# One layer of a hybrid gated-DeltaNet / GLA trunk on one core: weight block sums made by accumulating transfers, and a decay gate in one pass

## The chip, the cores and the metric

The kernel runs on one core of a Trainium2 chip. The metric is the device time of one execution in microseconds (us), the median of several runs. The engines are named as the profile names them: PE is TensorE (PEld its weight loads), DVE is VectorE, ACT is ScalarE, POOL is GpSimd, SP is SyncE, whose queue issues most transfers.

## The reference, cut to what matters

One layer over 1024 frames of width 1024, all in fp32. One input projection feeds two branches, and only the second one's gate is written out here:

```python
h = rmsnorm(x, norm_mix_g)                      # (1024, 1024)
# w_in: columns of every head group
gdn: q, k, v, z, decay, beta                    # gated DeltaNet, 8 heads of 128
gla: q, k (4 heads of 128), v, r (4 heads of 256), low (rank 16)
merge gates: two of width 1024
...
gk = log_sigmoid(low @ gla_w_gate2 + bias) / 16 # the decay gate, (1024, 512)
o_gla = gla_chunked(q, k, v, gk)                # a scan over chunks of the state
x += merge(gdn, gla) @ w_out
x += cross_attention(x, mem)                    # 4 heads, 256 memory tokens
x += relu(rmsnorm(x) @ w1) ** 2 @ w2
```

Most of the arithmetic is in plain matrix products: the input projection, the output projections, and the two of the MLP.

## The kernel before, in words

An fp32 product is made of three single-pass matmuls (`mm3`, L582, L584, L586): each operand is split into a high part, which ACT rounds off (L622), and a low part, the difference, which DVE or POOL makes (L623); the passes are high by high, high by low and low by high. Where a matmul takes fp32 operands as they are, TensorE makes several passes of it by itself (L1067 in the decay gate, L1138 to L1142 in the scan).

Large dense products are also cut into 2 x 2 blocks and made with seven block products in place of eight (`wino`, `gla_dense`). The activations' block sums are made once (`bs`). The weights' block sums are made again for every weight unit, that is for every 256 columns of a weight: two `raw` tiles hold its blocks A11, A12, A21, A22, each of 128 x 512 elements, and `wino_w` adds and subtracts blocks in place (L1751, L1752, L1754, L1756), on POOL in the code. A planner may give such an instruction to DVE, and mostly does. Each of the seven operands is split into a tile of the ring `wop`, which has four tiles (RING). Twelve matmuls make one block product on 512 columns: four tiles of the contraction by three passes.

The stage that the change is about is `phase_gla`, the gated heads' stage, from about 100 to 650 us. For each of four heads it projects q, k, v and r, and makes the decay gate (`gla_gate`: one product of rank 16, as two matmuls of 512 columns, and then a log-sigmoid and a running sum), the scores (`gla_scores`), the scan over eight chunks (`gla_scan`), the norm and the output. Between these the code takes steps from a queue of dense products (`push`, `fill`, `until`; FA to FJ say how many), which hold the head's own projections and also the DeltaNet heads' q, k, v and z, by the table EXTRA. The DeltaNet stage follows, from about 650 to 1105 us, with dense products between its steps too (FILL, TFILL, SFILL).

The order on each engine is not the code's: the planner orders all instructions by a cost table, and the DMA queues' too. Every engine then works through its own list and waits where an operand or a buffer is not ready. The scan's squares (L1152) write to the tile `th`, of which there is one buffer, and keep only the sum. `pd` and `ps` are four banks each of the matmul accumulator; `ex` and `dx` are rows of 128 x 1024.

Of the kernel before, what the change touches and what calls it, by code (L numbers as in the profile page):

```python
# [11 lines left out]
F32 = mybir.dt.float32  # L12
# [6 lines left out]
P = 128  # L19
D = 1024  # L20
T = 1024
# [45 lines left out]
EXTRA = (('v', 'k', 't', 'q'), ('v', 't', 'k', 'q'), ('v', 't', 'k', 'q'), ('v', 't', 'k', 'q'))  # L67
QB, FOLDB = 2, 1
SFILL, PFILL, TFILL = 5, (2, 12), (4, 14, 0, 8, 10, 10)
FILL = ((7,), ('z0', 6, 10, 'z6', 'Q2'), (9, 'O1', 'z5', 'z3', 'Q3', 'z1'), ('z2', 'z4', 14, 'O0', 11, 'O3', 'z7', 8, 'Q1'), ('O2', 13, 'Q0', 12))  # L70
LASTG = (15, 5)
LAYP = (('PF', 8192, 1), ('k1', 4096, 2), ('NT1', 4096, 2), ('NT0', 4096, 2), ('Pm', 4096, 1), ('dm', 4096, 2), ('k0', 4096, 2), ('kdt0', 4096, 2), ('kdt1', 4096, 2), ('pr', 1024, 1), ('q', 4096, 2))
LAYQ = (('AT', 4096, 2), ('v0', 4096, 2), ('acc', 2048, 2), ('sz', 2048, 2), ('v1', 4096, 2), ('X', 4096, 2))
# [15 lines left out]
class Op:  # L89
# [7 lines left out]
    def __init__(self, ins, flex):  # L97
# [33 lines left out]
        if ins.opcode == "DMACopy":  # L131
            self.dma, self.cost, self.own, self.lat = True, ISSUE, LAND, LAND
            self.bytes = n * 4 * outs[0].ap[0][1]
            if ins_[0].bass_ap.tensor.name in HEADIN:
# [366 lines left out]
class Layer:  # L501
# [428 lines left out]
    def joined(self, dest, done=None, scale=1.0):  # L930

        nc = self.nc

        def put(b, pt):
            nc.scalar.activation(dest(*b), pt, AF.Copy, scale=scale)  # L935

        def add(b, pt):
            o = dest(*b)
            if scale == 1.0:
                nc.vector.tensor_tensor(o, pt, o, ADD)  # L940
            else:
                nc.vector.scalar_tensor_tensor(o, pt, scale, o, MUL, ADD)
# [12 lines left out]
        return evict  # L955

    def gla_dense(self, evicts, after=None):

        n, ws = self.wino_w(range(7), GLOV)
        yield  # L960
        bank = self.banks(2)
        for p in range(7):
            if p == 3:
                self.fetch_w()
# [18 lines left out]
    def gla_qk(self, sp):  # L983
        qk = [self.til(sp, [P, T], "qk", bufs=2) for _ in range(2)]
        return qk, self.joined(lambda i, half: qk[i][:, half * HALF:(half + 1) * HALF], None, float(P) ** -0.25)

    def push_gla_v(self, sp, h):

        v = [self.til(sp, [P, NB, 256], "v", bufs=2) for _ in range(2)]

        def dest(e):
            return lambda i, half: v[i][:, 4 * half + 2 * e:4 * half + 2 * e + 2].rearrange("p a b -> p (a b)")

        self.push(f"v{h}", self.gla_dense([[self.joined(dest(e)) for e in range(2)]]))
        return v

    def push_gla_r(self, sp, h, after=None):

        nc = self.nc
        sr = [self.dxt(sp) for _ in range(2)]  # L1000

        def done(j, half, o, x):
            nc.scalar.activation(o, x, AF.Silu)

        self.push(f"r{h}", self.gla_dense([self.joined(lambda j, half: sr[j][:, half * HALF:(half + 1) * HALF], done)],
                                          after))
        return sr

    def push_pair(self, sp, x, after=None):
# [8 lines left out]
        def done(i, half, o, x_):  # L1018
            nc.scalar.activation(o, x_, AF.Silu)
            nc.sync.dma_start(self.gd["z", u][i][:, half * HALF:(half + 1) * HALF], o)  # L1020

        self.push(x, self.gla_dense([self.joined(dest, done)], after))

    def push_qv(self, sp, which, u, after=None):
# [9 lines left out]
        def done(i, half, o, src):  # L1034
            if o is not src:
                nc.scalar.activation(o, src, AF.Copy)
# [19 lines left out]
        self.push(f"g{which}{u}", self.gla_dense([self.joined(dest, done)], after))  # L1056
        return turn()

    def gla_gate(self, sp, h):
        nc = self.nc  # L1060
        w2 = self.til(sp, [96, P], "w2g", bufs=1)
        nc.sync.dma_start(w2, self.a["w2g"][:, h * P:(h + 1) * P])
        zb = self.ext(sp)
        for half in range(2):
            s = slice(half * HALF, (half + 1) * HALF)
            pt = self.pss()
            nc.tensor.matmul(pt, w2, self.sm[:96, s], start=True, stop=True)  # L1067
# [121 lines left out]
    def queue_gla(self):  # L1189
# [5 lines left out]
        for h in range(LH):  # L1195
# [3 lines left out]
            q += [[a[f"w_g{x}"][h] if len(x) == 1 else a["w_gz"][int(x[1])]]  # L1199
# [3 lines left out]
    def phase_gla(self):  # L1203
        nc, a = self.nc, self.a
        with ExitStack() as ctx:
            sp = self.pool(ctx, "pgla", "right", bufs=2)
            self.bs[3] = self.late_h(self.t1d, lambda: self.ext(sp))
            sm = self.sm = self.til(sp, [P, T], "sm", bufs=1)
            g4 = self.dxt(sp)

            def done(i, half, o, x):
                if i == 1:
                    nc.scalar.activation(o, x, AF.Tanh, scale=0.5)
# [4 lines left out]
                                                        done), ev]))  # L1218
            self.until("u0")
            v = self.push_gla_v(sp, 0)  # L1220
# [506 lines left out]
    def fetch_w(self):  # L1727
# [3 lines left out]
        n, srcs = self.wq.popleft()  # L1731
        rs = []
        for src in srcs:
            rs.append([self.til(self.wp, [P, n, 256], "raw", bufs=RAWS) for _ in src])
            for t, x in zip(rs[-1], src):
                self.load(t, x)
        self.wr.append((n, rs))

    def wino_w(self, order, lov):
# [4 lines left out]
        n, rs = self.wr.popleft()  # L1744
# [627 lines left out]

def _rows(w, n):
# [5 lines left out]
def _layout(i):  # L2379
# [8 lines left out]
    A["w_lqk"] = _pairs(w[:, np.concatenate([np.concatenate([lq[h * P:(h + 1) * P], lk[h * P:(h + 1) * P]])  # L2388
                                             for h in range(LH)])])
    A["w_lv"] = _pairs(w[:, lv])  # L2390
    A["w_lr"] = _pairs(w[:, lr])
    for x, c in (("k", gk), ("q", gq), ("z", gz), ("v", gv)):
        A[f"w_g{x}"] = _pairs(w[:, c])

    gate = np.concatenate([ta, tb])
    A["w_gate"] = _units(w, gate, 16)
    sg = np.zeros((D, 256), w.dtype)
    sg[:, 0:8], sg[:, 32:40], sg[:, 64:80], sg[:, P:] = w[:, ga], w[:, gb], w[:, lg], w[:, gate[4 * P:5 * P]]
    A["w_gzd"] = _units(w, gz, 8)
    A["w_sg"] = _pairs(sg)  # L2400
    w2g = np.zeros((96, 512), w.dtype)
    w2g[64:80] = i["gla_w_gate2"][0]
# [58 lines left out]
```

## Time and profile before

| | |
|---|---|
| time, median of three runs | 2117.42 us (2116.35 to 2118.87) |
| profiled execution | 2117.52 us, of which its span is 2115.8 us |
| granted TensorE clock | 0.999 |
| busy, share of the span | PE 99%, PEld 84%, DVE 75%, ACT 57%, POOL 7% |
| DMA queues | 329.50 MB in 158235 packets, a mean of 156 GB/s |

A row of busy times gives, for each engine, the microseconds in which it worked and the count of its instructions. A row of waits reads: the engine that waited, the tile and line that it was about to work on, the engine, tile and line that it waited for, the total in us, how many times, and the longest. A row of a group gives line, engine, operation, output tile, input tiles and shape, the count, busy us, mean ns of one, the idle time ahead of it and what ended that. A row of the timeline begins with start and duration in us. Matmuls are pipelined, so the distance between two starts, not the duration, is what one costs.

### The profile page before, as it was taken

What the parts mean: (1) busy time and instruction counts of PE and PEld (TensorE: products, weight loads), DVE (VectorE), ACT (ScalarE), POOL (GpSimd) and SP (SyncE); (2) the same over time, 40 slices, a digit from 0 to 9 for tenths busy, and PEclk for the clock granted to TensorE, in tenths of its full rate; (3) what the DMA queues carried; (4) which work ended last, traced back from release to release, by engine and by line L of the source; (5) the groups of instructions that cost most, each with busy time, mean ns of one, the idle gap of its engine ahead of it and who ended that gap; (6) DMA issues with size and microseconds to landing.
All of it is one profiled execution on the core that took longest, in us unless ns stands there. A gap on an engine that the chain in (4) does not pass through costs nothing. (4 is left out here: it accounts for less than half of the span.)

```text
span 2115.8 us, 30952 instructions
## 1 busy us (share of the span) xinstructions
PE 2095.9 (99%) x10946; PEld 1783.7 (84%) x10946; DVE 1591.4 (75%) x2824; ACT 1210.2 (57%) x2390; POOL 158.3 (7%) x175
## 2 busy tenths in 40 slices
PE   8999999999999999999999999999999999999998
PEld 8889888898888899889888888888788888888887
DVE  8858888848776978787569999479967567567755
ACT  7446666637646586665655456566755557444433
POOL 0000001000001323231000000000100000000000
PEclk9999999999999999999999999999999999999999
DMA  8322232312325344554587752226444447778752
GB/s 329 129 71 63 90 106 83 93 61 95 100 95 199 116 133 135 187 171 140 176 281 244 257 169 88 90 73 221 137 146 141 156 151 213 220 250 293 248 180 100
DMA packets 158235, 329.50 MB, mean 156 GB/s; under 512 B 17016, under 2 KB 25592, under 8 KB 158080
## 3 DMA queue, kind: packets, MB, share of 16 engines
q1 hardware_dynamic: 157936, 327.50, 46.8%
q8 instruction: 86, 1.41, 0.3%
q14 instruction: 69, 0.57, 0.1%
q10 hardware_dynamic: 144, 0.03, 0.0%
HBM read 227.29 MB, written 100.17 MB: 155 GB/s over the span
## 5 line engine op out<-in xcount | busy, mean ns | idle before, releaser
L622 ACT ACTIVATE wop<-raw 128x512 fp32r<-128x512 f32 (+1 forms) x520 | 337.9, 654 | 431.4 <-PE pd L586 191.7
L623 DVE TENSOR_TENSOR wop<-raw,wop 128x512 fp32r<-128x512 f32 (+1 forms) x496 | 348.6, 706 | 232.3 <-ACT wop L622 224.7
L582 PE MATMUL pd<-t,wop 128*128 128x512 f32 x332 | 130.3, 393 | 0.5 <-ACT t L622 0.5
L586 PE MATMUL pd<-t,wop 128*128 128x512 f32 x332 | 130.4, 393 | 0.0
L584 PE MATMUL pd<-t,wop 128*128 128x512 f32 x332 | 130.2, 392 | 0.0
L584 PE MATMUL pd<-A1b,wop 128*128 128x512 f32 x272 | 106.3, 391 | 0.0
L582 PE MATMUL pd<-A1b,wop 128*128 128x512 f32 x272 | 105.9, 390 | 0.0
L586 PE MATMUL pd<-A1b,wop 128*128 128x512 f32 x260 | 101.2, 390 | 0.0
L1269 DVE SCALAR_TENSOR_TENSOR dx<-dx,convw,dx 128x1023 f32<-128x1023 f32 (+2 forms) x72 | 90.8, 1278 | 2.8 <-ACT dx L1267 2.5
L584 PE MATMUL pd<-A1a,wop 128*128 128x512 f32 x208 | 81.7, 393 | 0.0
L582 PE MATMUL pd<-A1a,wop 128*128 128x512 f32 x208 | 81.4, 391 | 0.0
L586 PE MATMUL pd<-A1a,wop 128*128 128x512 f32 x196 | 76.8, 392 | 0.0
L582 PEld LDWEIGHTS pd<-t,wop 128*128 128x128 f32 x332 | 62.3, 188 | 14.0 <-ACT t L622 0.9
L584 PEld LDWEIGHTS pd<-t,wop 128*128 128x128 f32 x332 | 62.4, 188 | 13.1 <-DVE t L623 0.4
L586 PEld LDWEIGHTS pd<-t,wop 128*128 128x128 f32 x332 | 62.4, 188 | 12.8
L622 ACT ACTIVATE whi<-raw 128x512 fp32r<-128x512 f32 x70 | 43.0, 626 | 34.8 <-PE pd L584 12.7
L582 PEld LDWEIGHTS pd<-A1b,wop 128*128 128x128 f32 x272 | 51.1, 188 | 10.7 <-ACT wop L622 0.3
L584 PEld LDWEIGHTS pd<-A1b,wop 128*128 128x128 f32 x272 | 51.1, 188 | 10.6 <-DVE A1b L623 0.2
L586 PEld LDWEIGHTS pd<-A1b,wop 128*128 128x128 f32 x260 | 48.8, 188 | 9.9
L623 DVE TENSOR_TENSOR wlo<-raw,whi 128x512 fp32r<-128x512 f32 x66 | 45.2, 685 | 14.3 <-ACT whi L622 12.3
L582 PEld LDWEIGHTS pd<-A1a,wop 128*128 128x128 f32 x208 | 39.1, 188 | 8.3 <-ACT dx L935 0.3
L584 PEld LDWEIGHTS pd<-A1a,wop 128*128 128x128 f32 x208 | 39.1, 188 | 8.0
(646 smaller groups left out, 6502.3 us busy)
## 6 DMA issues: line engine op xcount, KB each, us to landing
raw<-in_w_dram SPq DMA_DIRECT2D x120, 256.0 KB, 3.6
raw<-in_w_dram SPq DMA_DIRECT2D x32, 512.0 KB, 3.7
e<-ad SPq DMA_DIRECT2D x63, 256.0 KB, 4.6
ad<-q SPq DMA_DIRECT2D x45, 256.0 KB, 2.7
rawa<-ad SPq DMA_DIRECT2D x42, 256.0 KB, 4.4
A0b<-tgd SPq DMA_DIRECT2D x32, 256.0 KB, 5.2
ad<-acc SPq DMA_DIRECT2D x30, 256.0 KB, 2.3
ad<-u SPq DMA_DIRECT2D x30, 256.0 KB, 2.6
```

Source lines behind the costliest of these rows:

```text
L582: nc.tensor.matmul(out, lh, rh, start=first and i == 0, stop=False, skip_group_check=True)
L584: nc.tensor.matmul(out, lh, rl, start=False, stop=False, skip_group_check=True)
L586: nc.tensor.matmul(out, ll, rh, start=False, stop=last and i == n - 1, skip_group_check=True)
L622: nc.scalar.activation(hi, raw, AF.Copy)
L623: (lo_eng or nc.gpsimd).tensor_tensor(lo, raw, hi.bitcast(F32), SUB)
L1269: self.nc.vector.scalar_tensor_tensor(y[:, d:], x[:, :T - d], cw[:, 3 - d:4 - d], y[:, d:], MUL, ADD)
```

## The change

It has two parts, and numbers that were set anew with them.

First, in `phase_gla` the weights' block sums are made by transfers. `gla_w` takes the place of `wino_w` there: a block is read from memory a second time, by a transfer that POOL's queue issues and that adds to what stands in the tile. The sums that are wanted are now sums only: A21 becomes A21 + A22, then + A11, then + A12, and A11 becomes A11 + A21, in the order of products 0, 1, 3, 2, 4, 5, 6. The signs that this needs are put into the splits of products 2, 3 and 6 (ACT with a scale of -1, DVE with a scalar_tensor_tensor), and the lower halves of the outputs come out negated, which the evictions turn round (`low`). The weights are laid out by blocks in memory (`_blocks`), so that a block is one contiguous run in each partition. The product stages outside `phase_gla` keep `wino_w`.

Second, the decay gate's product: `low` holds the low-rank rows three times, in rows 48, 64 and 96, where the projection's weight (`w_sg`) has them three times. One copy of them is made a low part (rows 32 to 64 less their rounded value), two stay rounded; the gate's weight `w2` has the rounded value in rows 48 and 64 and its low part in row 96. So one single-pass matmul over 128 rows adds up low by high, high by high and high by low. `w2` is loaded into the tile `th`, and then copied and subtracted.

Third, FD, FH, FJ, EXTRA, SFILL, TFILL, FILL, LASTG, LAYP and LAYQ (fill numbers, the order of dense products, and the layout of two pools) have new values. `push_pair` can also make the merge gates, but EXTRA does not use that.

```diff
-FA, FB, FC, FD, FE, FG, FH, FI = 23, 31, 30, 20, 47, 24, 2, 0
+FA, FB, FC, FD, FE, FG, FH, FI = 23, 31, 30, 28, 47, 24, 0, 0
-FJ = 12
+FJ = 24
-EXTRA = (('v', 'k', 't', 'q'), ('v', 't', 'k', 'q'), ('v', 't', 'k', 'q'), ('v', 't', 'k', 'q'))
+EXTRA = (('v', 'k', 't', 'q'), ('v', 't', 'k', 'q'), ('k', 'v', 't', 'q'), ('k', 'v', 't', 'q'))
...
-    def joined(self, dest, done=None, scale=1.0):
+    def joined(self, dest, done=None, scale=1.0, low=1.0):
...
-            nc.scalar.activation(dest(*b), pt, AF.Copy, scale=scale)
+            nc.scalar.activation(dest(*b), pt, AF.Copy, scale=scale * (low if b[0] else 1.0))
...
+            elif f == -1.0:
+                nc.vector.tensor_tensor(o, o, pt, SUB)
...
+    SUMS = (0, 1, 3, 2, 4, 5, 6)
+
+    def gla_w(self):
...
+        more = lambda dst, src: nc.gpsimd.dma_start(dst, src, accum_op=ADD)
+        for p in self.SUMS:
+            for o, (a, src) in zip(ops, bl):
+                A11, A12, A21, A22 = a
+                if p == 0:
+                    more(A21, src[3])
...
+                w, (hi, lo) = (A11, A12, A21, A21, A11, A21, A22)[p], o[p]
+                if p in (2, 3, 6):
+                    nc.scalar.activation(hi, w, AF.Copy, scale=-1.0)
+                    nc.vector.scalar_tensor_tensor(lo, w, -1.0, hi.bitcast(F32), MUL, SUB)
+                else:
+                    self.split(w, hi, lo, nc.vector if p in GLOV else None)
+                if p in (0, 2, 3):
+                    more(*{0: (A11, src[2]), 3: (A21, src[0]), 2: (A21, src[1])}[p])
+        return n, ops
...
-        n, ws = self.wino_w(range(7), GLOV)
+        n, ws = self.gla_w()
...
     def gla_gate(self, sp, h):
         nc = self.nc
-        w2 = self.til(sp, [96, P], "w2g", bufs=1)
-        nc.sync.dma_start(w2, self.a["w2g"][:, h * P:(h + 1) * P])
+        raw = self.til(self.tp, [P, HALF], "th", bufs=THB)[:, :P]
+        nc.sync.dma_start(raw, self.a["w2g"][:, h * P:(h + 1) * P])
+        w2 = self.til(sp, [P, P], "w2g", F32R, bufs=1)
+        nc.scalar.activation(w2, raw, AF.Copy)
+        nc.vector.tensor_tensor(w2[96:], raw[96:], w2[96:].bitcast(F32), SUB)
...
-            nc.tensor.matmul(pt, w2, self.sm[:96, s], start=True, stop=True)
+            nc.tensor.matmul(pt, w2, self.low[:, s], start=True, stop=True)
...
-            sm = self.sm = self.til(sp, [P, T], "sm", bufs=1)
+            sm = self.sm = self.dxt(sp)
+            self.low = self.til(sp, [P, T], "sm", F32R, bufs=1)
...
+            nc.scalar.activation(self.low, sm, AF.Copy)
+            nc.vector.tensor_tensor(self.low[32:64], sm[32:64], self.low[32:64].bitcast(F32), SUB)
```

What this moves is seen at three places. In these rows a line is that of its own kernel (L622 of before is L624 of after, L623 is L625, L582 is L584, L1067 is L1111), and numbers behind a tile's name only tell its instances apart. The first place is DVE in head 2, where the q and k weights are split and summed (`raw`, `wop`), with the DeltaNet heads' convolution (`dx`) between. Before:

```order
L1752 TENSOR_TENSOR raw_3643<-raw_3643 128x4x128
L623 TENSOR_TENSOR wop_3722<-raw_3644,wop_3722 128x512
L1104 COPY ge_3865<-ex_3251 128x8
L1756 TENSOR_TENSOR raw_3644<-raw_3644,raw_3643 128x4x128
L940 TENSOR_TENSOR dx_3614<-pd_3647,dx_3614 128x512
L623 TENSOR_TENSOR wop_3727<-raw_3643,wop_3727 128x512
L1269 SCALAR_TENSOR_TENSOR dx_3688<-dx_3614,convw_194,dx_3688 128x1023
L623 TENSOR_TENSOR wop_3730<-raw_3643,wop_3730 128x512
L1269 SCALAR_TENSOR_TENSOR dx_3688<-dx_3614,convw_194,dx_3688 128x1022
L1754 TENSOR_TENSOR raw_3643<-raw_3644,raw_3643 128x4x128
```

After, for the same unit, products 3, 2 and then 4 and 5:

```order
L987 SCALAR_TENSOR_TENSOR wop_3739<-raw_3657,wop_3739 128x512
L1316 SCALAR_TENSOR_TENSOR dx_3700<-dx_3626,convw_194,dx_3700 128x1023
L1316 SCALAR_TENSOR_TENSOR dx_3700<-dx_3626,convw_194,dx_3700 128x1022
L1316 SCALAR_TENSOR_TENSOR dx_3700<-dx_3626,convw_194,dx_3700 128x1021
L1316 SCALAR_TENSOR_TENSOR dx_3722<-dx_3655,convw_194,dx_3722 128x1023
L1316 SCALAR_TENSOR_TENSOR dx_3722<-dx_3655,convw_194,dx_3722 128x1022
L987 SCALAR_TENSOR_TENSOR wop_3743<-raw_3657,wop_3743 128x512
L625 TENSOR_TENSOR wop_3747<-raw_3657,wop_3747 128x512
L946 SCALAR_TENSOR_TENSOR qk_3239<-pd_3770,qk_3239 128x512
```

The sums on `raw` (L1752, L1754, L1756) are gone from DVE, and the splits that wait for transfers (L987) stand there with other work between them. The second place is POOL's list, over the same part of the stage and a little around it. Before:

```order
L1756 TENSOR_TENSOR raw_3334<-raw_3334,raw_3333 128x4x128
L1751 TENSOR_TENSOR raw_3500<-raw_3500,raw_3501 128x4x128
L623 TENSOR_TENSOR wop_3441<-raw_3333,wop_3441 128x512
L1121 MEMSET ex_3848 64x4x64 x2
L1124 AFFINE_SELECT ex_3848<-ex_3848 128x512 x2
```

After, with the transfers of two weight units interleaved:

```order
L625 TENSOR_TENSOR wop_3450<-raw_3348,wop_3450 128x512
L972 DMA raw_3347<-in_w_gk_dram 128x512 x2
L972 DMA raw_3514<-in_w_gq_dram 128x512 x2
L972 DMA raw_3657<-in_w_lqk_dram 128x512
L972 DMA raw_3514<-in_w_gq_dram 128x512
L972 DMA raw_3657<-in_w_lqk_dram 128x512 x3
L972 DMA raw_3798<-in_w_lv_dram 128x1024
```

Where POOL had one block operation now and then, its list now holds four transfers for each unit, 92 in all, each of which waits in the list for the split ahead of it. The third place is PE at the decay gate of head 1, right behind the scan of head 0. Before, from the scan's last two matmuls, with ten dense matmuls up to the gate:

```order
L1140 MATMUL ps_2246<-v_1532,ex_1692 128x256
L1142 MATMUL ps_2246<-S_2237,qk_1281 128x256
L586 MATMUL pd_2040<-t_154_1159,wop_2037 128x512
L582 MATMUL pd_2040<-t_154_1159,wop_2037 128x512
L584 MATMUL pd_2040<-t_154_1159,wop_2037 128x512
L586 MATMUL pd_2040<-t_154_1159,wop_2037 128x512
L582 MATMUL pd_2040<-t_154_1159,wop_2037 128x512
L584 MATMUL pd_2040<-t_154_1159,wop_2037 128x512
L586 MATMUL pd_2040<-t_154_1159,wop_2037 128x512
L582 MATMUL pd_2040<-t_154_1159,wop_2037 128x512
L584 MATMUL pd_2040<-t_154_1159,wop_2037 128x512
L586 MATMUL pd_2040<-t_154_1159,wop_2037 128x512
```

```order
L1067 MATMUL ps_2278<-sm_1279,w2g_2275 128x512
L1067 MATMUL ps_2281<-sm_1279,w2g_2275 128x512
L582 MATMUL pd_2329<-A0a_202,wop_2304 128x512
L584 MATMUL pd_2329<-A0a_202,wop_2304 128x512
L586 MATMUL pd_2329<-A0a_202,wop_2304 128x512
```

After, the last rows ahead of the gate, and the gate:

```order
L588 MATMUL pd_2046<-t_154_1159,wop_2043 128x512
L584 MATMUL pd_2338<-A0a_202,wop_2314 128x512
L586 MATMUL pd_2338<-A0a_202,wop_2314 128x512
L588 MATMUL pd_2338<-A0a_202,wop_2314 128x512
L584 MATMUL pd_2338<-A0a_202,wop_2314 128x512
L1111 MATMUL ps_2287<-sm_1280,w2g_2283 128x512
L1111 MATMUL ps_2290<-sm_1280,w2g_2283 128x512
L586 MATMUL pd_2338<-A0a_202,wop_2314 128x512
```

The gate stands 28 dense matmuls behind the scan now (10 before), four of which already belong to the next product (`pd_2338`), and its two rows are of the single-pass kind.

More of the change, by code (lines that the diff above doesn't have):

```diff
@@ L992, in dest @@
             return lambda i, half: v[i][:, 4 * half + 2 * e:4 * half + 2 * e + 2].rearrange("p a b -> p (a b)")
-        self.push(f"v{h}", self.gla_dense([[self.joined(dest(e)) for e in range(2)]]))
+        self.push(f"v{h}", self.gla_dense([[self.joined(dest(e), None, 1.0, -1.0) for e in range(2)]]))
         return v
@@ L1002, in done @@
         def done(j, half, o, x):
-            nc.scalar.activation(o, x, AF.Silu)
-        self.push(f"r{h}", self.gla_dense([self.joined(lambda j, half: sr[j][:, half * HALF:(half + 1) * HALF], done)],
-                                          after))
+            nc.scalar.activation(o, x, AF.Silu, scale=1.0 if x is o else -1.0)
+        self.push(f"r{h}", self.gla_dense([self.joined(lambda j, half: sr[j][:, half * HALF:(half + 1) * HALF], done,
+                                                       1.0, -1.0)], after))
         return sr
@@ L1018, in done @@
         def done(i, half, o, x_):
-            nc.scalar.activation(o, x_, AF.Silu)
-            nc.sync.dma_start(self.gd["z", u][i][:, half * HALF:(half + 1) * HALF], o)
-        self.push(x, self.gla_dense([self.joined(dest, done)], after))
+            f = 1.0 if x_ is o else -1.0
+            if x[0] == "z":
+                nc.scalar.activation(o, x_, AF.Silu, scale=f)
+            else:
+                nc.scalar.activation(o, x_, AF.Tanh, scale=0.5 * f)
+            nc.sync.dma_start((self.gd["z", u][i] if x[0] == "z" else self.tgd[2 * u + i])[:, half * HALF:(half + 1) * HALF], o)
+        self.push(x, self.gla_dense([self.joined(dest, done, 1.0, -1.0)], after))
     def push_qv(self, sp, which, u, after=None):
@@ L1054, in turn @@
                     yield
-        self.push(f"g{which}{u}", self.gla_dense([self.joined(dest, done)], after))
+        self.push(f"g{which}{u}", self.gla_dense([self.joined(dest, done, 1.0, -1.0)], after))
         return turn()
@@ L1731, in fetch_w @@
         n, srcs = self.wq.popleft()
+        srcs = [[x for x in src] for src in srcs]
         rs = []
         for src in srcs:
-            rs.append([self.til(self.wp, [P, n, 256], "raw", bufs=RAWS) for _ in src])
+            rs.append([self.til(self.wp, list(x.shape), "raw", bufs=RAWS) for x in src])
             for t, x in zip(rs[-1], src):
                 self.load(t, x)
-        self.wr.append((n, rs))
+        self.wr.append((n, rs, srcs))
     def wino_w(self, order, lov):
```

66 lines of the change are left out of this document (43 added, 23 removed).

## The prediction

> **What bounds the kernel now.** I read the page first, then PE's list of waits, then the stretches by window.
>
> ```profile
> span 2115.8 us, 30952 instructions
> PE 2095.9 (99%) x10946; PEld 1783.7 (84%) x10946; DVE 1591.4 (75%) x2824; ACT 1210.2 (57%) x2390; POOL 158.3 (7%) x175
> ```
>
> PE is busy 2095.9 of 2115.8 us; every other engine has room. The profiled execution took 2117.52 us, so 1.7 us lie outside its span; it stands 0.1 us from the median of the three runs (2117.42), so what I subtract from the one can be subtracted from the other. The list of PE's waits says where the 20 us without a matmul are:
>
> ```profile
> PE pd L582 <- ACT mT L736: 5.6, 1, 5.6
> PE ps L1443 <- DVE NT L1366: 1.5, 1, 1.5
> PE pd L582 <- ACT q L935: 1.4, 1, 1.4
> PE ps L1443 <- ACT PF L1431: 1.3, 1, 1.3
> ```
>
> The largest is the start of the program. None lies in the stage that is changed: by the windows (PE's busy time is the first pair behind the length, then PEld, DVE, ACT, POOL, the granted clock, the DMA share and GB/s), PE is busy in all of 100 to 650 us, the gated heads' stage, and misses 4.87 us in 650 to 1105, the DeltaNet stage. The third row is a stretch of plain dense products.
>
> ```profile
> 100.00:650.00 550.00, 550.00 (x2973) 469.51 (x2972) 420.77 (x608) 325.21 (x521) 24.80 (x30) 1.00 0.26 85
> 650.00:1105.00 455.00, 450.13 (x2880) 397.35 (x2878) 343.81 (x807) 286.50 (x797) 95.90 (x116) 1.00 0.52 173
> 1150.00:1200.00 50.00, 50.00 (x222) 41.42 (x221) 44.85 (x74) 21.38 (x38) 0.00 (x0) 1.00 0.69 226
> ```
>
> 222 matmuls in 50 us are 0.225 us each (0.227 to 0.23 between neighbours in the timelines below). So in the changed stage time goes down only if PE has less to do, and goes up as soon as PE has to wait.
>
> **Part 1: the block sums leave DVE and POOL.** These rows are the sums of the gated heads' stage on DVE (line, out<-in, count, busy us, mean ns, idle before):
>
> ```profile
> L1754 DVE TENSOR_TENSOR raw<-raw,raw 128x512 f32<-128x512 f32 x21 | 14.3, 685 | 0.1
> L1756 DVE TENSOR_TENSOR raw<-raw,raw 128x512 f32<-128x512 f32 x20 | 13.6, 683 | 0.2
> L1752 DVE TENSOR_TENSOR raw<-raw 128x512 f32<-128x512 f32 x18 | 13.1, 726 | 0.1
> L1751 DVE TENSOR_TENSOR raw<-raw,raw 128x512 f32<-128x512 f32 x17 | 11.6, 682 | 0.0
> L1754 DVE TENSOR_TENSOR raw<-raw,raw 128x1024 f32<-128x1024 f32 x2 | 2.4, 1220 | 0.0
> ```
>
> With eight wide ones of 1.2 us, two in each of four lines, that is 52.6 + 9.8 = 62 us off an engine that is busy 421 of these 550 us. Since PE never waits here, I cost this at nothing: 62 us of DVE buy no time. The signs that the new order of products wants (a scale on an ACT copy, a subtraction for an addition) ride on instructions that exist already: nothing.
>
> **Part 2: 92 accumulating transfers take their place.** The trace of before holds no accumulating transfer. What has to fit: a weight unit makes seven products of 12 matmuls, 12 x 0.227 = 2.7 us each, and its split blocks go through a ring of four. In the new order (0, 1, 3, 2, 4, 5, 6) product 3's split is followed by a transfer, product 2's split waits for that and is followed by another, product 5's split waits for that one. Product 3's tile comes free when the product two ahead of the unit's first has ended, and product 5 is needed six products later: 6 x 2.72 = 16.3 us. Three splits lie in it,
>
> ```profile
> L622 ACT ACTIVATE wop<-raw 128x512 fp32r<-128x512 f32 (+1 forms) x520 | 337.9, 654 | 431.4 <-PE pd L586 191.7
> L623 DVE TENSOR_TENSOR wop<-raw,wop 128x512 fp32r<-128x512 f32 (+1 forms) x496 | 348.6, 706 | 232.3 <-ACT wop L622 224.7
> ```
>
> each 0.65 + 0.71 = 1.36 us, so (16.3 - 4.1)/2 = 6.1 us are left for each transfer, from the end of the split ahead of it to its landing. Where gate or scan matmuls stand between the products there is more. Counting so through the order of the changed kernel, unit by unit, I get 5.9 to 6.4 us for seven of the 22 units, 6.9 to 8.1 for ten, over 10 for five; a unit that is late by so much stops PE by as much. A transfer of 5.5 us then costs nothing, 6.5 costs 2.4 us in all, 7.0 costs 9, 7.5 costs 18, 8 costs 31, and 9.6 costs 82. (The 191.7 us that ACT waits for PE in the first row is the ring being full: the operands are there before PE wants them.) The nearest rows are the landing of the weight loads in this stage, and what POOL takes for a block of this size (count, then ns at least, median and most) or for the worst one in the program:
>
> ```profile
> DMA to landing us min/median/max: 2.9/3.7/5.8
> L1751 POOL TENSOR_TENSOR raw<-raw,raw x4: 1296/1298/3832, 233.4 to 1601.3; 128x512 f32<-128x512 f32 x4
> L623 POOL TENSOR_TENSOR B1b<-q,B1b 128x512 fp32r<-128x512 f32 x1 | 7.0, 7023 | 67.9 <-ACT B1b L622 67.9
> ```
>
> From below 2.9 us (a plain landing, POOL's part free); from above 5.8 + 7.0 = 12.8 us (slowest landing behind POOL's slowest operation), where the loss would pass 150 us. I take the medians of the first two rows: 3.7 + 1.3 = 5.0 us. A block is half as large as a load (128x512 against 128x1024), and POOL has 24.8 us of work in these 550 us, so the typical case is nearer to 5.0 than to the ends. At 5.0 every unit has at least 0.9 us to spare, and the cost is nothing.
>
> [...]
>
> **Part 3: the decay gate.** Two fp32 matmuls a head become two of the single-pass kind. Timeline of head 1's gate (start, us, engine, line):
>
> ```profile
> 215.56 0.39 PE L586 MATMUL pd<-t,wop 128*128 128x512 f32 x1
> 215.78 1.88 PE L1067 MATMUL ps<-sm,w2g 96*128 96x512 f32 x4
> 217.10 0.80 PE L582 MATMUL pd<-A0a,wop 128*128 128x512 f32 x1
> 217.74 0.39 PE L584 MATMUL pd<-A0a,wop 128*128 128x512 f32 x1
> 217.97 0.40 PE L586 MATMUL pd<-A0a,wop 128*128 128x512 f32 x1
> ```
>
> The gate holds PE from 215.78 to the start of the next dense matmul, which is one spacing ahead of 217.74: 217.74 - 0.23 - 215.78 = 1.73 us. Two single passes take 2 x 0.227 = 0.45. That is 1.28 us a head, 5.1 us for four, all on PE and so all of it time.
>
> What it adds: `w2` is loaded into the one `th` buffer, which the scan's squares write, so in heads 1 to 3 the load can't start until the last square of the scan ahead has ended. Then come the landing, an ACT copy, a DVE subtraction, and the gate. End of the scan of head 0, and the rows that price the chain:
>
> ```profile
> 213.03 0.59 PE L1142 MATMUL ps<-S,qk 128*128 128x256 f32 x2
> 213.28 0.59 PE L586 MATMUL pd<-t,wop 128*128 128x512 f32 x1
> 214.51 0.19 ACT L1152 ACTIVATION_READ_ACCUMULATOR th<-v 128x1 f32 x1
> DMA to landing us min/median/max: 3.6/4.4/5.3
> L1327 ACT ACTIVATE jk<-ps 128x128 f32<-128x128 f32 x128 | 35.6, 278 | 10.7 <-PE ps L654 6.9
> L1366 DVE SCALAR_TENSOR_TENSOR NT<-ps,nb,dm 128x128 f32<-128x128 f32 x64 | 17.6, 341 | 2.1 <-ACT dm L1321 2.0
> ```
>
> The last square ends at 214.70, 1.2 us after PE is done with the scan (213.28 + 0.23). The landing is that of `w2g` in before, 4.4 at the median; copy and subtraction are 0.28 + 0.34, and 0.3 go to handing over: 1.2 + 4.4 + 0.9 = 6.5 us. The cover is what PE does between the scan's last matmul and the gate: 28 matmuls for head 1 (6.4 us), 6.1 for head 2 and 7.0 for head 3, by the same count. PE would wait 0.1 + 0.4 + 0 = 0.5 us; if copy and subtraction queue a little (DVE is busy 421 of 550 us) it is about 1 us, which I take. Bounds: 0 with a landing of 3.6, 1.0 + 1.3 + 0.4 = 2.7 with 5.3, some 4 with a busy DVE on top. Queued behind the load on SP are the weight loads of a later unit and the spills of the head's output, which have several us; behind the copy on ACT one eviction and the gate's own reads.
>
> **Part 4: fewer fillers in the scan.** The scan of heads 0 to 2 had two dense matmuls in each chunk, now none; head 3 had none before. Its chunks (second pair) against head 0's (first):
>
> ```profile
> 202.07 0.59 PE L1138 MATMUL ps<-v,ex 128*128 128x256 f32 x2
> 203.84 0.60 PE L1138 MATMUL ps<-v,ex 128*128 128x256 f32 x2
> 585.22 0.59 PE L1138 MATMUL ps<-v,ex 128*128 128x256 f32 x2
> 586.51 0.59 PE L1138 MATMUL ps<-v,ex 128*128 128x256 f32 x2
> ```
>
> 1.77 us less two fillers of 0.23 is 1.31, against 1.29 alone without a wait: 0.02 to 0.03 over 24 chunks, 0.6 us saved at most, and nothing lost. I take 0.5.
>
> **Part 5: the DeltaNet stage** is reordered a little by the retuned fill numbers, with the same PE work. It holds 4.87 us of idle PE; the largest pieces are the second and the fourth row of PE's list (1.5 and 1.3). Added up along the orders with the durations of the trace, PE work between a gram and its inverse changes from 57.4, 115.0, 69.3, 111.4 to 57.2, 115.7, 70.4, 106.6 us, and DVE work in the four chains from 40.4, 44.7, 33.1, 46.2 to 40.3, 50.9, 38.5, 43.7: no direction in it. I take 0, with bounds of 4.9 less and 4 more.
>
> **Sum.** -5.1 (gate) + 1.0 (wait for `w2`) - 0.5 (scan) + 0 + 0 = -4.6 us; from 2117.4, 2112.8 us.
>
> **The rivals.**
>
> *The transfers come late (slower).* POOL's part of a transfer is held up beside a running DVE: it takes the 3.8 us of the longest block sum in POOL's row instead of the median's 1.3, and the transfer 3.7 + 3.8 = 7.5. Then ten or so of the units are late and PE stops at product 5 or 2 of each for 18 us together: 2112.8 + 18 = 2131. It decides from 7.05 us on: there the loss of 9 us passes the gain of 4.6 and the bound of 4.2. The ACT queue makes it worse, since a split that waits there stands ahead of evictions. For it: the 7.0 us row, and a queue on POOL in which one transfer that waits holds the next. Against it: the median block sum on POOL takes 1.30 us with DVE three quarters busy. Chance 0.25.
>
> *The waits in the DeltaNet stage shrink too (faster still).* Its idle is made of single waits of 1.5 us at most on DVE or ACT; a shift by 1 to 2 us can take some away. Some 4 of 4.87 us: 2108.8. For it: the waits are short. Against: nothing in the new order aims at them. Chance 0.2.
>
> *The gain is eaten (no change).* The `w2` chain at its upper end (4 us) with a DeltaNet stage that loses 1 to 3: 2116.5. Also what is left if DVE's relief was meant as the gain. Chance 0.1.
>
> *The forecast*, 2110.5 to 2115: chance 0.45.
>
> **The numbers.** A measurement of this kernel can tell about 0.2%, 4.2 us, from no change: faster is below 2113.2, slower above 2121.6. The forecast lies just past the bound; of its 0.45 I put 0.32 below 2113.2 and 0.13 above. Faster: 0.32 + 0.2 = 0.52; same: 0.13 + 0.1 = 0.23; slower: 0.25. Range: below, all but the end of the faster rival, 2107 (0.05 left out); above, the rival with late transfers up to 7.25 us, about 13 us lost, 2126 (0.13 left out). The forecast and the faster rival alone lie in 2107 to 2115.
>
> **What would show it.** In the trace after: no `raw` sums on DVE, and DVE's busy time in the stage some 60 us lower with PE still at 100%. Gate pairs of 0.45 us. A wait of PE for DVE or ACT on `w2g` of under 1 us in heads 1 and 2. Landing of the `raw` transfers issued by POOL about 5 us behind the split: over 6.5 and PE's list shows waits for `wop` splits in this stage, many of them, and the forecast is wrong. The DeltaNet stage's idle within 3 us of 4.9; otherwise Part 5 is wrong.

## The result, and the profile after

The changed kernel takes 2168.4 us (2163.9 to 2169.7), the kernel before 2117.8 in the same series: 1.024 times as long, with a 95% interval of 1.022 to 1.025. The forecast was 2112.8 us, in a range from 2107 to 2126. It is slower by 51 us, and outside the range. Three single executions of the later series, of 2320, 3543 and 7519 us, were far slower than their neighbours and are in none of the times below. First the page after, then PE's list of waits in 100 to 740 us, then PE's busy time and the granted clock by window:

```profile
span 2167.8 us, 31186 instructions
PE 2112.3 (97%) x10938; PEld 1784.9 (82%) x10938; DVE 1540.3 (71%) x2744; ACT 1208.5 (56%) x2393; POOL 229.3 (11%) x260
```

```profile
PE pd L584 <- ACT wop L986: 10.9, 7, 2.9
PE pd L584 <- ACT dx L937: 6.6, 9, 2.2
PE pd L584 <- ACT wop L624: 4.9, 6, 1.3
PE pd L588 <- DVE wop L987: 2.4, 2, 1.6
PE pd L584 <- ACT qk L937: 2.1, 3, 0.7
```

```profile
100.00:650.00 550.00, 519.31 (x2770) 432.88 (x2769) 343.68 (x493) 298.92 (x484) 89.98 (x104) 0.99 0.50 118
650.00:1105.00 455.00, 448.49 (x2867) 396.01 (x2866) 342.73 (x797) 288.37 (x793) 101.52 (x125) 0.99 0.50 161
```

DVE is relieved as the change says (344 us in this window, 421 before), and PE, which had no gap in the stage, now waits there: for splits of weights (`wop`) and for evictions (`dx`, `qk`). The DeltaNet stage behind it loses about what it lost before (6.5 us of idle PE, 4.9 before, in windows that no longer hold quite the same work). So most of the loss is in the stage, and most of it is waiting; a part is the clock, which is granted at half in a few spells of 3.41 or 6.83 us (half-clock spells below). These rows sum up the accumulating transfers, by the weight that they read (duration on POOL in ns, least, median, most):

```profile
L972 POOL DMA_DIRECT2D raw<-in_w_lqk_dram x16: 865/875/897, 74.6 to 592.3; - x16
L972 POOL DMA_DIRECT2D raw<-in_w_gk_dram x16: 865/875/950, 211.1 to 641.3; - x16
DMA to landing us min/median/max: 3.6/4.1/6.7
```

A transfer by itself is shorter than forecast: 4.1 us in the median from its start to its landing, and 0.4 from the end of the split to a start that nothing holds up, against 5.0. Three of a unit's four transfers wait for a split; the first, A21 + A22, does not. What is wrong is seen on POOL's timeline. One stretch, with the splits on ACT and DVE and the matmul that waits for them:

```profile
282.45 0.88 POOL L972 DMA_DIRECT2D raw<-in_w_lqk_dram  x1 [6.44 <-DVE wop L625]
285.41 0.69 DVE L987 SCALAR_TENSOR_TENSOR wop<-raw,wop 128x512 fp32r<-128x512 f32 x1
289.02 0.88 POOL L972 DMA_DIRECT2D raw<-in_w_lr_dram  x1 [5.70 <-issue]
293.33 0.88 POOL L972 DMA_DIRECT2D raw<-in_w_lqk_dram  x1 [3.43 <-DVE dx L1316]
297.32 0.63 ACT L986 ACTIVATE wop<-raw 128x512 fp32r<-128x512 f32 x1 [5.55 <-DMA raw<-in_w_lqk_dram]
298.00 0.50 PE L584 MATMUL pd<-t,wop 128*128 128x512 f32 x1 [2.87 <-ACT wop L986]
```

The split at 285.41 ends at 286.10, and from then on the transfer that adds to its block could go. It goes at 293.33. Ahead of it in POOL's list stands a transfer of the next unit, whose result is first read by a split at 310; that one does not start until 289.02, 0.3 us after the transfer of 282.45 has landed, and the urgent one not until 0.3 us after that has landed. The brackets name what ended POOL's idle time as far as the profile can tell; "issue" means that it shows no wait there. The `dx` in the bracket of 293.33 is a neighbour in time and not the cause: with a larger descriptor store (below) the same transfer goes before that work on `dx`. In the whole trace no accumulating transfer starts while another is under way: of the 91 distances from a landing to the next start none is under 0.31 us, and 41 lie between 0.31 and 0.40. From the end of a split to the landing of its transfer, 69 times, it took 4.0 to 11.6 us, in the median 5.9; 30 of them took longer than the 6.1 us that the tightest units have, and 28 stood for over 1 us between the end of their split and their start.

### The profile page after: what moved, and what is told of

Same layout as the page of the kernel before. It is cut to its first block, busy times and chain, and to the rows that moved or that the text cites. A ratio compares the mean times of both kernels' runs of the same rounds, so it can differ in the third digit from the quotient of the medians.

```text
span 2167.8 us, 31186 instructions
## 1 busy us (share of the span) xinstructions
PE 2112.3 (97%) x10938; PEld 1784.9 (82%) x10938; DVE 1540.3 (71%) x2744; ACT 1208.5 (56%) x2393; POOL 229.3 (11%) x260
## 5 line engine op out<-in xcount | busy, mean ns | idle before, releaser
L624 ACT ACTIVATE wop<-raw 128x512 fp32r<-128x512 f32 (+1 forms) x451 | 291.5, 651 | 362.1 <-PE pd L588 157.5
L625 DVE TENSOR_TENSOR wop<-raw,wop 128x512 fp32r<-128x512 f32 (+1 forms) x428 | 298.9, 702 | 231.8 <-ACT wop L624 226.2
L584 PE MATMUL pd<-t,wop 128*128 128x512 f32 x332 | 133.6, 402 | 19.4 <-ACT wop L986 10.4
L588 PE MATMUL pd<-t,wop 128*128 128x512 f32 x332 | 132.1, 398 | 0.9 <-DVE wop L987 0.9
L586 PE MATMUL pd<-t,wop 128*128 128x512 f32 x332 | 131.6, 396 | 0.0
L584 PE MATMUL pd<-A1b,wop 128*128 128x512 f32 x272 | 106.4, 392 | 0.0
L584 PEld LDWEIGHTS pd<-t,wop 128*128 128x128 f32 x332 | 63.2, 190 | 41.2 <-ACT wop L986 13.3
L987 DVE SCALAR_TENSOR_TENSOR wop<-raw,wop 128x512 fp32r<-128x512 f32 (+1 forms) x69 | 50.8, 736 | 58.3 <-ACT wop L986 58.1
L584 PE MATMUL pd<-A1a,wop 128*128 128x512 f32 x208 | 82.0, 394 | 3.7 <-ACT wop L624 3.5
L624 ACT ACTIVATE whi<-raw 128x512 fp32r<-128x512 f32 x70 | 43.2, 628 | 41.6 <-PE pd L586 28.1
L584 PEld LDWEIGHTS pd<-A1b,wop 128*128 128x128 f32 x272 | 51.1, 188 | 10.6 <-ACT wop L624 0.3
L625 DVE TENSOR_TENSOR wlo<-raw,whi 128x512 fp32r<-128x512 f32 x64 | 43.6, 685 | 16.1 <-ACT whi L624 15.8
```

Of the source, the lines that this page charges most:

```text
L584: nc.tensor.matmul(out, lh, rh, start=first and i == 0, stop=False, skip_group_check=True)
L586: nc.tensor.matmul(out, lh, rl, start=False, stop=False, skip_group_check=True)
L588: nc.tensor.matmul(out, ll, rh, start=False, stop=last and i == n - 1, skip_group_check=True)
L624: nc.scalar.activation(hi, raw, AF.Copy)
L625: (lo_eng or nc.gpsimd).tensor_tensor(lo, raw, hi.bitcast(F32), SUB)
L987: nc.vector.scalar_tensor_tensor(lo, w, -1.0, hi.bitcast(F32), MUL, SUB)
```

## The experiments

Four questions: is it the gate, the new order, or the transfers; what about the transfers; what else is in the stage; and can the gate's saving be had alone.

**The gate alone** (before with `gla_gate`, `low` and the weights' rows of the change; the sums as before):

```diff
-        w2 = self.til(sp, [96, P], "w2g", bufs=1)
...
+            nc.tensor.matmul(pt, w2, self.low[:, s], start=True, stop=True)
```

> The kernel before with only the decay gate's part of the change (single-pass product of stacked parts, its weight loaded into the scan's scratch tile); block sums on the engines, fill numbers and block order as before. If the loss comes from the accumulating transfers, in whichever way, this gives what the gate was forecast to give: 2117.4 - 5.1 + up to 2.7 of waiting for the gate's weight = 2112 to 2115 us, gate pairs 0.45 us apart, no new wait of PE in 100 to 650 us. If the gate's part, with its load behind the scan, holds a share of the loss, 2118 us or more.

Measured: 2123.0 us, 1.002 times before (1.001 to 1.003). By the number this is the second side (2118 us or more): the saving is not there, and 4.6 us of the 51 are. But no wait for `w2g` is in PE's list, a gate pair takes 0.46 us, and the waits are for DVE and ACT at other places. In 100 to 650 us PE stands idle for 3.4 us; the wait of 2.2 us for `B1b` lies at 1108, and a half-clock spell of 3.41 us follows it (granted clock of the whole run 0.998, 0.999 before).

```profile
PE ps L582 <- ACT B1b L622: 2.2, 1, 2.2
PE ps L654 <- DVE ex L1176: 1.6, 1, 1.6
PE pd L586 <- DVE wop L623: 1.2, 1, 1.2
```

The planner orders every engine anew when an operation changes, and this order has waits that the old one had not. Whether the gate's own operations make them is decided by the last two runs.

**The sums on the engines** (changed kernel, the 92 transfers replaced):

```diff
-                    more(A21, src[3])
...
+                if p == 0:
+                    nc.gpsimd.tensor_tensor(A11, A11, A21, ADD)
+                    nc.gpsimd.tensor_tensor(A21, A21, A22, ADD)
+                if p == 3:
+                    nc.gpsimd.tensor_tensor(A21, A22, A11, ADD)
+                if p == 2:
+                    nc.gpsimd.tensor_tensor(A21, A21, A12, ADD)
```

> The changed kernel with the same block sums in the same order of products, made by DVE or POOL in place of the 92 accumulating transfers; gate, fill numbers, signs and weight layout as changed. If the transfers hold the loss (by their queue or by their length), PE's waits in the gated heads' stage go and with them the half-clock spells there: 2111 to 2117 us, of which up to 5 over the gate-only kernel for the DeltaNet stage's new order. If the new order of products, the fill numbers or the gate hold the loss, 2135 us or more.

Measured: 1.0045 times before (1.003 to 1.006), about 2128 us (three runs, 2124.9 to 2131.5), between the two sides. So 40 of the 51 us go with the transfers.

```profile
100.00:650.00 550.00, 547.44 (x2963) 466.18 (x2962) 429.22 (x618) 325.17 (x525) 23.40 (x25) 1.00 0.26 85
```

PE is idle for 2.6 us of this window, where it was idle for 30.7 in the changed kernel. The remaining 10 us over before, 15 over what the gate should give, come with the new order and fill numbers, more than expected, and for the larger part they do not lie in this window: the DeltaNet stage has 7.0 us of idle PE (4.9 before), and there are half-clock spells of 3.41 us at 997 and at 1953, the second behind a wait of 2.0 us (granted clock 0.998, 0.999 before).

**Plain transfers** (one word less, every list the same):

```diff
-        more = lambda dst, src: nc.gpsimd.dma_start(dst, src, accum_op=ADD)
+        more = lambda dst, src: nc.gpsimd.dma_start(dst, src)
```

> The changed kernel with plain transfers in place of accumulating ones: each block is loaded over the tile and nothing is added, so the sums are left out; every list of instructions is the same as in the changed kernel. Theory A, POOL's queue runs its transfers one at a time, whatever they do: each starts about 0.3 us after the one ahead has landed, as in the changed kernel, and the time stays within 15 us of 2168 (a landing may be some tenths shorter). Theory B, only accumulating transfers wait for each other: starts come before the landing ahead, several are in flight, PE's waits in the stage fall to a third or less, 2110 to 2130 us. Theory C, a transfer's own length is what is late and the queue is no matter: starts overlap or not, the time follows the landing alone.

Measured: 2140.3 us, 28 less than the changed kernel. Theory B's mechanism with a smaller gain than it gave. POOL's timeline, first of the changed kernel, then of this one, over the same transfers:

```profile
234.66 0.88 POOL L972 DMA_DIRECT2D raw<-in_w_gk_dram  x1 [7.10 <-DVE wop L625]
240.87 0.89 POOL L972 DMA_DIRECT2D raw<-in_w_gq_dram  x1 [5.34 <-issue]
245.05 0.88 POOL L972 DMA_DIRECT2D raw<-in_w_gk_dram  x1 [3.29 <-issue]
```

```profile
233.24 0.55 POOL L972 DMA_DIRECT2D raw<-in_w_gk_dram  x1 [7.46 <-DVE wop L625]
235.42 0.54 POOL L972 DMA_DIRECT2D raw<-in_w_gq_dram  x1 [1.63 <-DMA raw<-in_w_gq_dram]
238.12 0.54 POOL L972 DMA_DIRECT2D raw<-in_w_gk_dram  x1 [2.17 <-DVE wop L987]
DMA to landing us min/median/max: 2.7/3.2/5.8
```

They start when their own operands are ready: 32 of them before the one ahead has landed, three in flight at most. They also land sooner, at 3.2 us in the median.

**The first of four sums on the engines** (`more(A21, src[3])` as a `tensor_tensor`):

> The changed kernel with only the first of the four sums (A21 + A22, wanted last of all, 5 to 25 us after its landing) made by DVE or POOL; 69 transfers are left, among them both of the chain from product 3 over product 2 to product 5. If the loss comes from urgent transfers standing behind transfers that are not urgent, this takes most of it: 2113 to 2130 us. If the chain's own length is too long by itself (two landings and three splits), little changes: 2145 us or more.

Measured: 2140.8 us, 1.011 times before (1.009 to 1.012). Between the two: with a quarter of the transfers gone more than half of the loss is gone, but 23 us stay, so not being urgent is not all of it. (The expectation calls this sum the one wanted last; it is wanted by product 3, the third of seven. It is the one with the longest time between its landing and its use in most units, 7 us or more.)

**Plain, one at a time** (a wait added from each transfer on POOL to the landing of the one ahead):

> The plain transfers of the third experiment (sums left out, the same lists), but each on POOL's list is told to wait for the landing of the one ahead. If it is the one-at-a-time running that costs the 28 us between the plain transfers (2140) and the changed kernel (2168), most of it comes back: 2153 to 2168 us. If it is the 0.9 us by which an accumulating transfer lands later, or the adding itself, it stays at 2140 to 2145.

Measured: 2141.3 us. A miss for my theory: one at a time alone costs nothing here. These transfers hold the queue for 3.1 + 0.4 = 3.5 us each, the accumulating ones for 4.1 + 0.3 = 4.4. A unit has four, and seven products of 2.72 us, 19.1 us: four times 3.5 is 14.0 and leaves room, four times 4.4 is 17.6 and leaves next to none. It is the two together that cost, one at a time and 0.9 us longer; the next run gives the fourth corner. That the room in a unit is what decides is worked out from these numbers; no run had a length between the two.

**A larger descriptor store for POOL's transfers** (the room in each partition that the program sets aside for them, `dynamic_dma_scratch_size`), with the work of every engine as changed:

```diff
-        nc = bacc.Bacc("TRN2", target_bir_lowering=False, num_devices=1, dynamic_dma_scratch_size=512)
+        nc = bacc.Bacc("TRN2", target_bir_lowering=False, num_devices=1, dynamic_dma_scratch_size=1024)
...
-            jk = self.til(self.tp, [P, HALF], "th", bufs=THB)[:, :256]
+            jk = self.til(self.tp, [P, 256], "th", bufs=THB)
```

> The changed kernel with a descriptor store for POOL's transfers of 1024 bytes in each partition in place of 512 (the room comes from a smaller scratch tile, two pads and a constant moved into another tile). Theory R, the next transfer waits because the store has no room for its descriptors while the one ahead is under way: starts come before the landing ahead, two or three accumulating transfers are in flight, and the time comes near the plain transfers' 2140: 2135 to 2150 us. Theory U, accumulating transfers follow each other by their nature: every start still comes 0.3 us or more behind the landing ahead, 2160 to 2172 us.

Measured: 2141.1 us, 1.010 times before (1.009 to 1.012), 27 less than with 512 bytes. Theory R by its starts and its time. Every engine's list is that of the changed kernel, but for one fill of a constant on DVE. The same three transfers, then the split and the urgent transfer that stood at 285.41 and 293.33 above:

```profile
234.64 0.86 POOL L970 DMA_DIRECT2D raw<-in_w_gk_dram  x1 [7.18 <-DVE wop L625]
236.43 0.89 POOL L970 DMA_DIRECT2D raw<-in_w_gq_dram  x1 [0.93 <-DMA raw<-in_w_gq_dram]
239.55 0.88 POOL L970 DMA_DIRECT2D raw<-in_w_gk_dram  x1 [2.23 <-DVE wop L985]
DMA to landing us min/median/max: 3.6/4.4/8.3
280.53 0.69 DVE L985 SCALAR_TENSOR_TENSOR wop<-raw,wop 128x512 fp32r<-128x512 f32 x1
281.63 0.88 POOL L970 DMA_DIRECT2D raw<-in_w_lqk_dram  x1 [1.34 <-DVE wop L985]
```

The second starts at 236.43, with the first under way until past 238, and up to three are in flight. The urgent transfer goes 0.4 us after its split, where it took 7.2, and of the 69 transfers that follow a split 2 start more than 1 us behind it (28 before). So accumulating transfers can overlap, and the size of the store set how many were under way: with 512 bytes they went one at a time, where plain ones went up to three, and with 1024 bytes up to three of them. What of a transfer takes room in the store, and how many bytes, was not measured.

| | up to three under way | one at a time |
|---|---|---|
| plain, 3.1 to 3.2 us to landing | 2140.3 us | 2141.3 us |
| accumulating, 4.1 to 4.4 us | 2141.1 us | 2168.4 us |

**Another order of products**, and both together:

```diff
-    SUMS = (0, 1, 3, 2, 4, 5, 6)
+    SUMS, ALONE = (0, 1, 3, 2, 4, 5, 6), (0, 3, 2, 1, 4, 5, 6)
```

> The changed kernel with the products of the single weight units in the order 0, 3, 2, 1, 4, 5, 6 (double units keep 0, 1, 3, 2, 4, 5, 6). Products 2 and 4, which add up in the same bank with an eviction between, stand side by side at nine places of the changed kernel's list on PE, where PE waits 0.85 us each for the eviction; here product 1 stands between them, and product 5's chain has one product more, 2.7 us. If both count: 9 x 0.85 = 8 us less, and up to 15 more from the chain, 2145 to 2160 us. If the queue alone decides, 2160 us or more.

> Both: the store of 1024 bytes and the order 0, 3, 2, 1, 4, 5, 6. If the two causes are separate, the gains add: 2168 - 20 to 28 - 8 to 15 = 2125 to 2140 us, near the kernel with the sums on the engines (2126). If they are the same waits seen twice, no better than the better of the two alone.

Measured: the order alone 2175.3 us, 7 us worse than the changed kernel. By the number this is the second side (2160 us or more), but neither side had it slower than the changed kernel. Together with the larger store: 2137.0 us, 1.009 times before (1.007 to 1.010), 4 us better than the store alone. The nine waits of 0.85 us that the order was to remove are real: with the larger store and the old order they stand clear in PE's list, and with the new order only single waits are left.

```profile
PE pd L584 <- ACT dx L935: 5.1, 9, 1.0
PE pd L584 <- ACT qk L935: 2.1, 3, 0.7
```

```profile
PE pd L584 <- ACT dx L935: 5.8, 1, 5.8
PE pd L588 <- DVE wop L985: 2.2, 2, 1.7
```

The first list (larger store) holds the nine, six of them for `dx` and three for `qk`, and three more of another kind; one such place in the changed kernel reads

```profile
385.55 0.39 PE L588 MATMUL pd<-t,wop 128*128 128x512 f32 x1
385.98 0.60 ACT L937 ACTIVATE dx<-pd 128x512 f32<-128x512 f32 x1 [1.22 <-PE pd L588]
386.63 0.50 PE L584 MATMUL pd<-t,wop 128*128 128x512 f32 x1 [0.69 <-ACT dx L937]
```

Product 2 ends, ACT evicts its bank, and product 4, which goes on adding in that bank, has to wait: 386.63 - 385.55 is 1.08 us where 0.23 is usual. The second list (both changes) has them no more, but one wait of 5.8 us for an eviction that stands behind other work on ACT. The order alone is worse while transfers go one at a time. PE's list there still has the splits behind transfers, two long waits for evictions, and, new, a scan's matmul that waits for DVE, on whose list a split that waits for a transfer can stand ahead of the scan. That this is the reason for the third row is argued, not shown.

```profile
PE pd L584 <- ACT wop L986: 9.6, 6, 3.6
PE pd L584 <- ACT dx L937: 8.9, 2, 6.4
PE ps L1187 <- DVE S L1193: 8.8, 2, 4.5
```

The clock adds to it: this kernel has nine half-clock spells ahead of its end, 37.5 us in all (granted clock 0.990), where the changed kernel has four, 17.1 us (0.995). At half clock this is up to 10 us more, against a difference of 7.

**The gate alone, in other orders** (two fill numbers, then six):

```diff
-FA, FB, FC, FD, FE, FG, FH, FI = 23, 31, 30, 20, 47, 24, 2, 0
+FA, FB, FC, FD, FE, FG, FH, FI = 23, 31, 30, 20, 47, 20, 0, 0
```

> The gate-only kernel with two fill numbers set anew (FG 24 to 20, FH 2 to 0). If the gate's saving of 5.1 us is real on PE and was eaten in the gate-only kernel by a few waits of its new order (3.1 us around 360 us, 2.4 and a half-clock spell at 1109), another order should give it back: 2111 to 2117 us, below the kernel before. If the gate's part itself makes the waits (its load behind the scan, the copy on ACT, the subtraction on DVE), they stay and the time is 2118 to 2124 us again.

> The gate-only kernel with other fill numbers (FC 24, FD 30, FE 41, FG 22, FH 1, FJ 52), so a third order of the same work: the spread between the three tells what the order alone is worth. 2111 to 2120 us if the gate's saving is kept; around 2122 if it is lost in any order.

Measured: 2113.1 us, 0.9974 times before (0.9965 to 0.9984), and 2113.8 us, 0.9979 (0.9970 to 0.9988), against 2118.2. Both beat both kernels, with the same gate as the gate-only kernel of 2123.0 us; so its waits came from its order. Page, window and the waits of the first in the two stages:

```profile
span 2111.1 us, 30963 instructions
100.00:650.00 550.00, 550.00 (x2986) 471.89 (x2985) 425.60 (x618) 328.50 (x528) 24.75 (x30) 1.00 0.26 86
PE pd L582 <- ACT t L622: 1.4, 1, 1.4
PE ps L1449 <- ACT PF L1437: 1.2, 1, 1.2
```

PE is busy in all of the stage again, and its span is 4.7 us shorter than before's: the gate's 5.1, nearly whole. Its gate in the timeline:

```profile
216.13 0.73 PE L1070 MATMUL ps<-sm,w2g 128*128 128x512 f32 x2
216.69 0.40 PE L584 MATMUL pd<-A0a,wop 128*128 128x512 f32 x1
```

216.69 - 216.13 is 0.56 us for the pair, where it was 1.73.

## Why the prediction was wrong, point by point

**Bounds.** Right, and it carries the rest: PE had no gap in the stage, so whatever makes PE wait there is time.

**Part 1, DVE's relief worth nothing: right.** By the page DVE works 51 us less in the whole program (77 in the window, which holds fewer instructions than before), and nothing is gained; the two fast gate-only kernels have DVE as busy as before and no wait of PE in the stage. But I priced only the signs that the new order wants, and not the order. Products 2 and 4 share an accumulator bank, and in the order 0, 1, 3, 2, 4, 5, 6 they are neighbours. PE waits for that at nine places of the changed kernel, most often for 0.85 us, 7.6 in all at this price. That could have been read beforehand, from the table of banks and the order.

**Part 2, the transfers: the step that failed.** The term was nothing; it measured about 40 us (2168 less 2128). The length that I put in, 5.0 us, was too long (4.1 and 0.4 ahead of it). I held each transfer alone, with one length for all, against its 6.1 us, and took it that the next can start while one is under way. They went one at a time, in the list's order, and four a unit fill 17.6 of 19.1 us. It is the spread that costs, 4.0 to 11.6 us from split to landing: by the prediction's own scale (5.5 us costs nothing, 6.5 costs 2.4) a median of 5.9 for all would have cost next to nothing. About 27 us of the 40 are the queue (2168 to 2141 with the larger store, every list the same). Some 7 of the remaining 13 are the nine evictions: in the kernel with sums on the engines matmuls of product 5 stand between the neighbours at all but one of them. With the larger store PE's list still has 6.5 us of waits for `wop` splits in 100 to 740 us, 4.2 of them in the rows of L984 and L985, the splits of products 2, 3 and 6; with the sums on the engines it has 0.8. That points to the transfers' own length for the rest. This division of the 13 us is read from the lists, and no run takes it apart.

**The slower rival had the right side and the wrong mechanism.** It gave 2131 us by POOL being held up beside DVE. POOL's part of a transfer took 0.87 to 1.07 us over all 92, with DVE busy for 344 of 550 us, so a hold of 2.5 us (the rival's 3.8 less 1.3) is not in it. Some landings took up to 2.6 us longer than the median, and no run says why. In the rival's text stood "a queue on POOL in which one transfer that waits holds the next", without a price. That was the cause.

**A second price that was left out: the clock.** Behind some of PE's waits the granted clock fell to half. The 3.41 us ahead of two such spells, then the first of the spells, and matmuls within it:

```profile
296.30:299.71 3.41, 1.71 (x6) 1.15 (x7) 1.29 (x2) 2.39 (x5) 0.62 (x1) 1.00 0.07 11
378.22:381.63 3.41, 1.70 (x7) 0.74 (x5) 3.41 (x9) 3.17 (x6) 0.00 (x0) 1.00 1.04 371
299.70:303.10 3.40, 2.85 (x7) 1.66 (x6) 0.00 (x0) 0.81 (x2) 0.25 (x1) 0.50 0.90 207
299.79 0.63 PE L584 MATMUL pd<-t,wop 128*128 128x512 f32 x1
300.21 0.63 PE L586 MATMUL pd<-t,wop 128*128 128x512 f32 x1
```

0.42 us a matmul in place of 0.23. The changed kernel has three spells of 3.41 us in the stage and one of 6.83 in the DeltaNet stage; the kernel with the larger store has none ahead of its end (granted clock 0.999, as before, against 0.995). Half of their time is at most 1.7 us each for the short ones and 3.4 for the long one, so up to 8.5 of the 27 us are this. In the 3.41 us ahead of each of the four PE stood idle for 1.7 to 2.0 us; but in the same trace it stood idle for 2.2 us of 273.40 to 276.80 and for 2.9 us of 611.60 to 615.00, and the clock is 1.00 in the 3.40 us behind either, so not every such wait is followed by a spell. What sets the clock back was not shown.

**Part 3, the gate: right in size.** 5.1 us was forecast and the two runs with other fill numbers gave 5.1 and 4.4 (2118.2 less 2113.1 and 2113.8). The wait for `w2`, put at 1.0 us, hardly came: the gate pairs of heads 1 and 3 take 0.57 us in the changed kernel in place of 0.46, and no row of PE's list names `w2g`. The 0.3 us for handing over from engine to engine was my estimate; at head 3's gate the first matmul starts 0.05 us behind the subtraction (512.06, after 511.72 + 0.29). Its load landed in 1.8 to 2.0 us, not in 4.4.

```profile
L1103 SPq DMA_DIRECT2D th<-in_w2g_dram x4: 327/328/368, 99.7 to 506.1; - x4
DMA to landing us min/median/max: 1.8/1.9/2.0
```

**Parts 4 and 5.** 0.5 us in the scan is within what cannot be told. The new order was costed at nothing in the DeltaNet stage, with bounds from 4.9 less to 4 more; what new orders do in the whole kernel is larger. The gate alone in three orders took 2123.0, 2113.1 and 2113.8 us, and the new order with the sums on the engines, 2128 us, stands 15 above the gate's 2113.

## What to carry to other kernels

A new kind of transfer is priced as a queue, not as a latency: how many go through it in the time of one unit, how long each holds it, whether two can be under way at once, and what stands ahead of the urgent one (here four a unit, 4.4 us each, one at a time, in 19.1 us). When the order of accumulations changes, look which neighbours now share a bank with an eviction between them (most often 0.85 us at nine places here). A saving that is all on the bounding engine vanished in one replanned order here and came back in two others, so a change is judged over a few orders.

## What the runs showed of the hardware that was not expected

With a descriptor store of 512 bytes a partition, accumulating transfers of 128 rows from POOL's queue ran one at a time (next start at least 0.31 us behind the landing), plain ones up to three at a time; with 1024 bytes up to three accumulating ones. An accumulating transfer of 128x512 held POOL for 0.88 us and landed in the median after 4.1 us, a plain one for 0.54 and 3.2. In the changed kernel 1.7 to 2.0 us of idle PE within 3.41 us were followed four times by a half-clock spell: three of 3.41 us, up to 1.7 us more each, and one of 6.83; 2.2 and 2.9 us of it, once each, were not.
